# Two transformer layers on one core: transposing queries and keys by block, and moving the buffers of some gated pairs

## The chip, the core and the metric

The kernel runs on one core of a Trainium2 chip. The metric is the device time of one execution in microseconds, and the time before is the median of three. The engines named below are TensorE (PE), VectorE (DVE), ScalarE (ACT), GpSimd (POOL) and SyncE (SP), which issues the large loads.

## What is computed

Two layers over 256 tokens of width 1024, each of a feed-forward half-step, three groups of attention heads side by side, and a second feed-forward half-step, all with scales, shifts and gates from a conditioning vector. Cut to what matters:

```python
def swiglu(h, w_gu, w_down):
    g, u = jnp.split(h @ w_gu, 2, axis=-1)
    return (jax.nn.silu(g) * u) @ w_down

for l in range(DEPTH):                                    # 2
    mod = cond @ w_mod[l] + b_mod[l]
    sh1, sc1, g1, sh2, sc2, g2, sh3, sc3, g3 = jnp.split(mod, 9, axis=-1)
    h = modulate(x, norm_g[l, 0], sh1, sc1)
    x = x + 0.5 * g1[:, None, :] * swiglu(h, w_ffn1_gu[l], w_ffn1_down[l])     # 2 x 2816 wide
    h = modulate(x, norm_g[l, 1], sh2, sc2)
    c_q, c_kv, k_pe, q_s, k_s, v_s, qkv_sb = _split_cols(h @ w_in[l], IN_SIZES)
    qa = (rms_norm(c_q, q_a_norm[l]) @ w_uq[l]).reshape(B, S, MLA_HEADS, MLA_QK)    # 6 heads of 64 + 32
    qa = rms_norm(qa, mla_q_norm[l])
    qa = jnp.concatenate([qa[..., :MLA_NOPE], rope(qa[..., MLA_NOPE:], positions)], axis=-1)
    kv = (rms_norm(c_kv, kv_a_norm[l]) @ w_ukv[l]).reshape(B, S, MLA_HEADS, MLA_NOPE + MLA_V)
    ...                                                   # ka likewise, its rotated part shared by the heads
    o_a = mla_attention(qa, ka, va)
    ...                                                   # o_b: sliding window, o_c: stick-breaking
    x = x + g2[:, None, :] * (mix @ w_out[l])
    h = modulate(x, norm_g[l, 2], sh3, sc3)
    x = x + 0.5 * g3[:, None, :] * swiglu(h, w_ffn2_gu[l], w_ffn2_down[l])
```

## The kernel before

**Matmuls.** Every large product is made of three (`mm3`, L243, L246 and L247): weights and activations are split into a high and a low part (`hi`, `lo`; `h_hi`, `h_lo`), and high x high, high x low and low x high are added up in PSUM. Each is 128x128 weights by 256 tokens, or 258 with two more columns for a shift. ScalarE rounds a loaded weight chunk to its high part (L230), VectorE subtracts to get the low one (L234). PSUM has eight banks, four under the tag `mm` (`pmm`) and four under `acc` (`pacc`).

**Order.** The program is written as generators that advance one another; a scheduler then sets each engine's order from the dependencies. `pin` holds an instruction in the order in which it was written relative to the other pinned ones of its engine. Some orders are written out as numbers (`C`, L27).

**Feed-forward.** There are four such blocks, called FFN 1 to FFN 4 here (two in each layer). The width of 2816 makes 11 pairs j = 0 to 10. A pair's up-projection is gated into a tile `g`, with a high and a low part for two times 128 features, and the down-projection reads it into `acc` banks. The tiles come from the pool `g_p` with three buffers. FFN 1 alone starts with `up_first`, which takes four pairs at once, one eighth of the input width at a time (eight k-steps), since the conditioning vector's scale and shift for each eighth are only then worked out by `opening`: L454 multiplies by the norm's scale, L171 (in `mod_tile`, two for each step) makes scale and shift with L157 and L163 behind it, L460 and L461 on ScalarE apply them and round to `h_hi`, L462 on VectorE gives `h_lo`. Only then can TensorE do the 48 matmuls of the step. Pairs 2 and 3 of FFN 1 lie in two further buffers of their own (`more["g"]`). The other three blocks start with `up_unscaled`, which takes pair 0 on the input before its scale is known, with 258 columns. Between its pairs FFN 1 also makes the table of position biases, with small matmuls at L613.

**Attention.** In each layer the first head group (MLA) makes queries by two matmuls for each block of 128 tokens and three heads (L863), ScalarE and VectorE copy and rotate them into `qcat` (L866, L835 to L838), and VectorE scales the keys from four `mm` banks (`kps`) into `kcat` (L879, L880). Then 24 transposes by TensorE (L900), of 128 tokens by 96, go by twos of heads into an `mm` bank for both blocks; ScalarE copies the queries to `qT` (L903), VectorE the keys to `kT` (L905), 96x512 at a time. Beside it `qv`, a norm of the queries, goes through VectorE (L884), POOL's power (L886) and VectorE again (L888). TensorE has the 258-column matmuls of the next head group (`unscaled`) to go on with, and L1058 makes the scores from `kT` and `qT`. The mixed heads lie in the tiles `mid` until the output projection reads them.

## Time and profile before

| | |
|---|---|
| median of three executions | 1006.03 us (1005.33, 1006.03, 1011.27) |
| the profiled execution | 1007.52 us |
| its span, first to last instruction | 1005.6 us |
| TensorE busy | 983.7 us, 98% of the span |
| VectorE, ScalarE, POOL busy | 792.2, 533.3 and 76.6 us |
| mean granted clock of TensorE | 0.998 |
| read from memory | 242.69 MB, 242 GB/s over the span |

Matmuls are pipelined: one of 256 columns is shown with 0.28 us, and the next starts before it ends. A busy TensorE therefore says nothing of the pace; the number of instructions in a stretch does. The engine's share of busy time is high throughout, so single waits of one or two microseconds are looked for in the order of time.

### The profile page before, as it was taken

Reading aid. Unit: us, or ns where it says so; the run is one execution under the profiler, and the core shown is the slowest. Engines: PE = TensorE matmul, PEld = TensorE weight load, DVE = VectorE, ACT = ScalarE, POOL = GpSimd, SP = SyncE. Lnnn points to the kernel's source line nnn. Section 1 sums busy time; section 2 is a strip of 40 time slices with the busy share of each in tenths; the row PEclk is TensorE's granted clock in tenths of the full one; section 3 lists DMA queues with packets and bytes.
Section 4 is the critical chain, followed back from the end, with each engine's and each line's share of the span. In section 5 each row is a group of like instructions: output and inputs, shape, how many; then the busy total and the mean of one; then the engine's idle time right before and its main releaser. Section 6 shows DMA issues by size and latency. Waiting matters only on the chain.

```text
span 1005.6 us, 20450 instructions
## 1 busy us (share of the span) xinstructions
PE 983.7 (98%) x8396; PEld 957.1 (95%) x8396; DVE 792.2 (79%) x1422; ACT 533.3 (53%) x951; POOL 76.6 (8%) x123
## 2 busy tenths in 40 slices
PE   7999999998999999999999999999999999999998
PEld 6999999997888999999999999999988899999998
DVE  6999788898886898888789877777886678566663
ACT  4464345465755764444376444446575666444442
POOL 6001503002010000000000000000110000000000
PEclk9999999999999999999999999999999999999999
DMA  9988998654661679888866887772443146566631
GB/s 347 414 299 340 296 371 329 271 189 137 224 238 49 244 275 394 340 354 339 348 217 240 335 300 295 273 285 95 127 146 112 58 181 240 194 228 248 224 114 43
DMA packets 47936, 245.13 MB, mean 244 GB/s; under 512 B 4193, under 2 KB 4961, under 8 KB 29666
## 3 DMA queue, kind: packets, MB, share of 16 engines
q1 hardware_dynamic: 47840, 243.81, 64.9%
q8 instruction: 66, 1.08, 0.4%
q14 instruction: 28, 0.23, 0.1%
q10 hardware_dynamic: 2, 0.00, 0.0%
HBM read 242.69 MB, written 1.11 MB: 242 GB/s over the span
## 4 chain that ended last, share of the span: by engine, by line
PE 88%; DVE 7%; ACT 3%; POOL 1%; issue 1%; ACTq 0%; DVEq 0%; POOLq 0%
PE mm L243 16%; PE mm L246 16%; PE mm L247 16%; PE acc L246 11%; PE acc L243 11%; PE acc L247 11%; DVE lo L234 2%; DVE raw L171 1%; PE mm L1102 1%; PE mm L1082 1%; POOL qv L886 1%; PE mm L797 1%; PE mm L613 0%; PE mm L944 0%; PE mm L1143 0%
## 5 line engine op out<-in xcount | busy, mean ns | idle before, releaser
L234 DVE TENSOR_TENSOR lo<-raw,hi 128x1024 fp32r<-128x1024 f32 (+2 forms) x312 | 372.8, 1211 | 115.2 <-ACT hi L230 114.8
L230 ACT ACTIVATE hi<-raw 128x1024 fp32r<-128x1024 f32 (+1 forms) x296 | 306.5, 1048 | 201.9 <-PE mm L246 126.9
L246 PE MATMUL mm<-h_lo,hi 128*128 128x256 f32 (+1 forms) x1360 | 377.1, 278 | 0.0
L243 PE MATMUL mm<-h_hi,hi 128*128 128x256 f32 (+1 forms) x1360 | 376.8, 278 | 0.0
L247 PE MATMUL mm<-h_hi,lo 128*128 128x256 f32 (+1 forms) x1360 | 375.4, 277 | 0.0
L246 PEld LDWEIGHTS mm<-h_lo,hi 128*128 128x128 f32 x1360 | 254.8, 187 | 0.1
L243 PEld LDWEIGHTS mm<-h_hi,hi 128*128 128x128 f32 x1360 | 254.4, 188 | 0.3 <-ACT bias L620 0.2
L247 PEld LDWEIGHTS mm<-h_hi,lo 128*128 128x128 f32 x1360 | 254.0, 187 | 0.2
L243 PE MATMUL acc<-g,hi 128*128 128x256 f32 x682 | 188.9, 277 | 0.0
L247 PE MATMUL acc<-g,lo 128*128 128x256 f32 x682 | 188.9, 277 | 0.0
L246 PE MATMUL acc<-g,hi 128*128 128x256 f32 x682 | 188.7, 277 | 0.0
L171 DVE CUSTOM_DVE_ANT_0 raw<-raw,cond 128x1024 f32<-128x1024 f32 x144 | 172.2, 1220 | 0.0
L247 PEld LDWEIGHTS acc<-g,lo 128*128 128x128 f32 x682 | 128.2, 188 | 0.1
L243 PEld LDWEIGHTS acc<-g,hi 128*128 128x128 f32 x682 | 128.2, 188 | 0.0
L246 PEld LDWEIGHTS acc<-g,hi 128*128 128x128 f32 x682 | 128.0, 188 | 0.0
L243 PE MATMUL acc<-h_hi,hi 128*128 128x256 f32 (+1 forms) x288 | 79.8, 291 | 4.5 <-ACT h_hi L461 1.7
L246 PE MATMUL acc<-h_lo,hi 128*128 128x256 f32 (+1 forms) x288 | 80.5, 285 | 0.2
L247 PE MATMUL acc<-h_hi,lo 128*128 128x256 f32 (+1 forms) x288 | 79.3, 283 | 0.0
L448 ACT ACTIVATE g<-gg 128x256 fp32r<-128x256 f32 x82 | 34.0, 417 | 60.9 <-DVE gg L447 60.8
L445 ACT ACTIVATE sg<-mm 128x256 f32<-128x256 f32 x78 | 29.4, 377 | 59.5 <-PE mm L247 58.9
L243 PEld LDWEIGHTS acc<-h_hi,hi 128*128 128x128 f32 x288 | 53.2, 191 | 6.3 <-ACT h_hi L461 1.9
L246 PEld LDWEIGHTS acc<-h_lo,hi 128*128 128x128 f32 x288 | 54.9, 192 | 0.9 <-DVE h_lo L732 0.6
(307 smaller groups left out, 1122.8 us busy)
## 6 DMA issues: line engine op xcount, KB each, us to landing
raw<-in_dram SPq DMA_DIRECT2D x218, 1024.0 KB, 6.1
raw<-in_dram SPq DMA_DIRECT2D x4, 832.0 KB, 7.3
raw<-in_dram SPq DMA_DIRECT2D x4, 768.0 KB, 4.7
raw<-in_dram SPq DMA_DIRECT2D x4, 512.0 KB, 6.7
far<-relm SPq DMA_DIRECT2D x8, 256.0 KB, 11.4
small<-in_dram SPq DMA_DIRECT2D x2, 960.0 KB, 6.0
xT<-in_dram SPq DMA_DIRECT2D x4, 256.0 KB, 4.2
out_dram<-xT SPq DMA_DIRECT2D x3, 256.0 KB, 2.3
```

The lines of the kernel that those rows point to most:

```text
L171: return DVE.tensor_tensor_reduce(w, w, cond, 1.0, 0.0, ALU.mult, ALU.add, modc[:, l, v, d:d + 1])
L230: t = DVE.tensor_copy(hi, r) if on[i:i + 1] == "d" else ACT.activation(hi, r, AF.Copy)
L234: t = DVE.tensor_tensor(lo, r, hi.bitcast(F32), op=ALU.subtract)
L243: t = PE.matmul(o, wh, ah, start=start, stop=False)
L246: PE.matmul(o, wh, al, start=False, stop=False)
L247: PE.matmul(o, wl, ah, start=False, stop=stop)
L445: ACT.activation(sg, banks[t][:, 0:T], AF.Silu)
L448: behind[0] = ACT.activation(g[:, 0], gg, AF.Copy).ins
L797: PE.matmul(kp[:, 0:384], cT[:, 2, b * P:(b + 1) * P], wukv[:, hf * 384:(hf + 1) * 384], start=True, stop=True)
L886: POOL.tensor_tensor(rq, qv, nhalf[:, 0:12].rearrange("p (a b) -> p a b", a=2), op=ALU.pow)
L1082: PE.matmul(opv[:, i * 64:(i + 1) * 64], pT[:, j * P:(j + 1) * P], va[:, kb, h0 + i], start=kb == 0, stop=kb == b)
L1102: PE.matmul(sp[:, i * P:(i + 1) * P], win["q"][rr, i, b * P:(b + 1) * P], ksT[rr, kb * P:(kb + 1) * P], start=True, stop=True)
```

## The change

It has four parts. In the feed-forward blocks the pool `g_p` has two buffers, not three, and every third pair (j = 0, 3, 6 and 9) lies in a tile `gm` that is 48 floats longer than needed: its data begin after 40 floats where it is j = 0 or FFN 1, else after 48. In the built program that is address 160416 or 160448 in each partition; the second is a multiple of 64, the first lies 32 beyond one. (Before, the three buffers were all at multiples of 64, the two of `more["g"]` 32 beyond; these two, which hold j = 2 and 3 of FFN 1, are so still.) In `opening` L454 is pinned. In attention `qcat` and `kcat` are made earlier in the program, `gr` has a tile of its own, and `lr`, `rk2` and `mx` share those that they are worked out from; through this other tiles move as well, `mid` from 32 beyond a multiple of 64 to a multiple of 64. And the transposes go by block and threes of heads, by the function `turned`: those of the queries into `acc` banks, called as each rotation but the first two has been written, the last two after a block's keys; those of the keys into `mm` banks as each block of `kcat` is written. A copy is then 96x3x128.

```diff
-    g_p = ctx.enter_context(tc.tile_pool(name="g", bufs=3))
+    g_p = ctx.enter_context(tc.tile_pool(name="g", bufs=2))
     act_p = ctx.enter_context(tc.tile_pool(name="act", bufs=1))
+    off_p = ctx.enter_context(tc.tile_pool(name="off", bufs=1))
...
+        def gated(j):
+
+            if j % 3:
+                return g_p.tile([P, 2, 2, T], F32R, tag="g0", name="g")
+            t = off_p.tile([P, 4 * T + 48], F32R, tag="gm", name="gm")
+            return t[:, 40 if start or j == 0 else 48:][:, 0:4 * T].rearrange("p (a b t) -> p a b t", a=2, b=2)
...
-            gt[f0 // 2] = g_p.tile([P, 2, 2, T], F32R, tag="g0", name="g")
+            gt[f0 // 2] = gated(f0 // 2)
...
-                    gt[f // 2] = (more["g"] if t >= 4 else g_p).tile([P, 2, 2, T], F32R, tag="g%d" % max(t - 3, 0), name="g")
+                    gt[f // 2] = more["g"].tile([P, 2, 2, T], F32R, tag="g%d" % (t - 3), name="g") if t >= 4 else gated(f // 2)
...
-            DVE.tensor_tensor(xa[:, d], xT[:, d], rb0, op=ALU.mult)
+            pin(DVE.tensor_tensor(xa[:, d], xT[:, d], rb0, op=ALU.mult))
...
-        gr = gv
+        gr = ap.tile([P, 2, 3], F32, name="gr")
...
+        qss = ap.tile([P, 2, 6], F32, name="qss")
+        kss = ap.tile([P, 2, 6], F32, name="kss")
+        qcat = ap.tile([P, 1536], F32, tag="s1", name="qcat")[:, 0:1152].rearrange("p (b h d) -> p b h d", b=2, h=6)
+        kcat = ap.tile([P, 1536], F32, tag="s2", name="kcat")[:, 0:1152].rearrange("p (b h d) -> p b h d", b=2, h=6)
         kpT = ap.tile([32, T], F32, name="kpT")
...
-        lr = ap.tile([P, 2, 2], F32, name="lr")
+        lr = lv
...
+        def turned(dst, src, b, hf, bank):
+
+            tp = bank()
+            for i in range(3):
+                PE.transpose(tp[0:96, i * P:(i + 1) * P], src[:, b, hf * 3 + i], ident)
+            o = dst[:, hf * 3:hf * 3 + 3, b * P:(b + 1) * P]
+            t3 = heads3(tp[0:96, 0:3 * P])
+            if dst is qT:
+                ACT.activation(o, t3, AF.Copy, scale=gq[0:96])
+            else:
+                DVE.tensor_copy(o, t3)
...
                 DVE.tensor_reduce(qss[:, b, hs], sq, axis=AX.X, op=ALU.add)
+                if 2 * b + hf > 1:
+                    turned(qT, qcat, b - 1, hf, pacc)
...
             DVE.tensor_tensor(kcat[:, b, :, 64:96], krs[b].to_broadcast([P, 6, 32]), spread(rk[:, b], 32), op=ALU.mult)
+            turned(qT, qcat, 1, b, pacc)
+            for hf in range(2):
+                turned(kT, kcat, b, hf, pmm)
...
-        for h2 in range(3):
-            for src, dst in ((qcat, qT), (kcat, kT)):
-                tp = pmm()
-                for i in range(2):
-                    for b in range(2):
-                        PE.transpose(tp[0:96, (i * 2 + b) * P:(i * 2 + b + 1) * P], src[:, b, h2 * 2 + i], ident)
...
-            rk2 = ap.tile([P, 4], F32, name="rk2")
+            rk2 = kv2
...
-        mx = ap.tile([P, 2, 6], F32, name="mx")
+        mx = nm
```

**VectorE in the opening, k-steps 1 and 2, before.** Lines of the kernel after lie 1 above those of the kernel before up to L366 and 8 above them in the feed-forward part: L171 becomes L172, L454 becomes L462 and L462 becomes L470.

```order
L454 TENSOR_TENSOR xa<-xT,rsb 128x256
L171 ISA raw,modc<-raw,cond 128x1024
L171 ISA modc 128x1
L171 ISA raw,modc<-raw,cond 128x1024
L171 ISA modc 128x1
L454 TENSOR_TENSOR xa<-xT,rsb 128x256
L157 TENSOR_TENSOR modc<-modc,cols 128x2
L454 TENSOR_TENSOR xa<-xT,rsb 128x256
L163 SCALAR_TENSOR_TENSOR modc<-modc,cols 128x1
L454 TENSOR_TENSOR xa<-xT,rsb 128x256 x4
L462 TENSOR_TENSOR h_lo<-xa,h_hi 128x256
```

And the same engine after, from the L158 of step 1 on:

```order
L158 TENSOR_TENSOR modc<-modc,cols 128x2
L164 SCALAR_TENSOR_TENSOR modc<-modc,cols 128x1
L470 TENSOR_TENSOR h_lo<-xa,h_hi 128x256
L235 TENSOR_TENSOR lo<-raw,hi 128x1024 x2
L462 TENSOR_TENSOR xa<-xT,rsb 128x256
L172 ISA raw,modc<-raw,cond 128x1024
L172 ISA modc 128x1
L172 ISA raw,modc<-raw,cond 128x1024
L172 ISA modc 128x1
```

The seven products L454 stood nearly together ahead of the first h_lo; now one stands in each step, behind h_lo and the two L235 and ahead of the next L172.

**TensorE in attention of layer 0, before,** from the last query matmuls to the first unscaled one:

```order
L863 MATMUL acc<-small,cT 128x288 x8
L900 MATMUL mm<-ident,qcat 96x128 x4
L900 MATMUL mm<-ident,kcat 96x128
L900 MATMUL mm<-ident,qcat 96x128 x3
L900 MATMUL mm<-ident,kcat 96x128 x3
L900 MATMUL mm<-ident,qcat 96x128
L900 MATMUL mm<-ident,kcat 96x128 x4
L900 MATMUL mm<-ident,qcat 96x128 x4
L900 MATMUL mm<-ident,kcat 96x128 x4
L243 MATMUL acc<-h_hi,hi 128x258
```

After, where L890 is the query matmul, L875 a transpose and L244 the unscaled matmul:

```order
L890 MATMUL acc<-small,cT 128x288 x6
L875 MATMUL acc<-ident,qcat 96x128 x3
L890 MATMUL acc<-small,cT 128x288 x2
L875 MATMUL acc<-ident,qcat 96x128 x9
L875 MATMUL mm<-ident,kcat 96x128 x12
L244 MATMUL acc<-h_hi,hi 128x258
```

The query transposes went into the query matmuls and behind them, into `acc` banks; the key transposes stand together.

**VectorE in attention of layer 1, before,** from the scaling of the keys to the copies of their transposes:

```order
L879 TENSOR_TENSOR kcat<-mm,rkn 128x3x64 x2
L880 TENSOR_TENSOR kcat<-kr,kv 128x6x32
L879 TENSOR_TENSOR kcat<-mm,rkn 128x3x64 x2
L880 TENSOR_TENSOR kcat<-kr,kv 128x6x32
L884 TENSOR_SCALAR qv<-qss,lr_9053 128x6 x2
L293 SCALAR_TENSOR_TENSOR h_lo<-xa,modc,h_hi 128x256
L888 TENSOR_SCALAR qv<-qv,lr 128x6 x2
L905 COPY kT<-mm 96x512 x3
```

After, where L908 and L909 scale the keys, L881 copies transposed keys, L916 and L920 handle `qv`:

```order
L908 TENSOR_TENSOR kcat<-mm,rkn 128x3x64
L909 TENSOR_TENSOR kcat<-kr,kv 128x6x32
L908 TENSOR_TENSOR kcat<-mm,rkn 128x3x64 x2
L881 COPY kT<-mm 96x3x128 x2
L909 TENSOR_TENSOR kcat<-kr,kv 128x6x32
L916 TENSOR_SCALAR qv<-qss,lr_9062 128x6 x2
L294 SCALAR_TENSOR_TENSOR h_lo<-xa,modc,h_hi 128x256
L920 TENSOR_SCALAR qv<-qv,lv 128x6
L881 COPY kT<-mm 96x3x128 x2
L920 TENSOR_SCALAR qv<-qv,lv 128x6
```

Two copies moved ahead of the second block's L909 (L880 before), the other two between the halves of L920, which stood ahead of all copies as L888.

## Rows read from the trace of the kernel before

**Rows 1.** The page: busy time, share of the span and number of instructions of each engine; the granted clock of TensorE in 40 equal slices of the span, in tenths of full speed; shares of the span by engine in the chain of work that ended last.

```profile
PE 983.7 (98%) x8396; PEld 957.1 (95%) x8396; DVE 792.2 (79%) x1422; ACT 533.3 (53%) x951; POOL 76.6 (8%) x123
...
PEclk9999999999999999999999999999999999999999
...
PE 88%; DVE 7%; ACT 3%; POOL 1%; issue 1%; ACTq 0%; DVEq 0%; POOLq 0%
```

**Rows 2.** Busy time of TensorE in nine stretches of the four feed-forward blocks, in which only 128x256 matmuls are issued. Columns: stretch; its length; busy time of TensorE and number of its instructions; granted clock; share of the DMA engines; GB/s. The first six lie in FFN 1, the others in FFN 2, 3 and 4.

```profile
33.00:53.00 20.00, 20.00 (x179) 1.00 1.03 415
61.00:81.00 20.00, 20.00 (x172) 1.00 0.67 242
87.10:98.10 11.00, 11.00 (x97) 1.00 0.86 313
110.00:130.00 20.00, 20.00 (x172) 1.00 1.03 306
147.00:157.00 10.00, 10.00 (x91) 1.00 0.76 287
171.00:191.00 20.00, 20.00 (x173) 1.00 0.87 351
371.00:391.00 20.00, 20.00 (x179) 1.00 0.96 372
555.00:575.00 20.00, 20.00 (x179) 1.00 0.88 343
857.00:877.00 20.00, 20.00 (x179) 1.00 0.56 205
```

**Rows 3.** Single instructions of TensorE in FFN 1, in order of time: start, duration, engine, line, operation, output and inputs, number; in brackets its idle time just before, and what ended it. The first four are of the opening k-steps, the last is of the bias table's matmuls.

```profile
23.06 0.38 PE L243 MATMUL acc<-h_hi,hi 128*128 128x256 f32 x1 [0.72 <-ACT hi L230]
...
30.76 0.50 PE L243 MATMUL acc<-h_hi,hi 128*128 128x256 f32 x2 [1.74 <-ACT h_hi L461]
...
53.55 0.37 PE L246 MATMUL acc<-h_lo,hi 128*128 128x256 f32 x1
...
59.40 0.38 PE L246 MATMUL acc<-h_lo,hi 128*128 128x256 f32 x1
...
143.75 0.88 PE L613 MATMUL mm<-steps,hot 128*128 128x24 bf16 x29
```

**Rows 4.** Single instructions of VectorE near the start, when L454 makes the products of the later k-steps.

```profile
20.07 0.42 DVE L454 TENSOR_TENSOR xa<-xT,rsb 128x256 f32<-128x256 f32 x1
...
20.89 1.42 DVE L454 TENSOR_TENSOR xa<-xT,rsb 128x256 f32<-128x256 f32 x4
22.24 0.41 DVE L462 TENSOR_TENSOR h_lo<-xa,h_hi 128x256 fp32r<-128x256 f32 x1
```

**Rows 5.** Single instructions of VectorE in one k-step of the opening, and the last h_lo.

```profile
38.41 0.16 DVE L163 SCALAR_TENSOR_TENSOR modc<-modc,cols 128x1 f32<-128x1 f32 x1
...
40.19 1.23 DVE L234 TENSOR_TENSOR lo<-raw,hi 128x1024 fp32r<-128x1024 f32 x1 [0.45 <-ACT hi L230]
41.33 0.42 DVE L462 TENSOR_TENSOR h_lo<-xa,h_hi 128x256 fp32r<-128x256 f32 x1
...
44.27 0.16 DVE L163 SCALAR_TENSOR_TENSOR modc<-modc,cols 128x1 f32<-128x1 f32 x1
...
58.92 0.42 DVE L462 TENSOR_TENSOR h_lo<-xa,h_hi 128x256 fp32r<-128x256 f32 x1
```

**Rows 6.** TensorE's instructions that read `mid`, in one stretch of each layer, with the columns of rows 2.

```profile
328.60:337.60 9.00, 9.00 (x78) 1.00 0.38 138
812.10:821.10 9.00, 9.00 (x78) 1.00 0.37 135
```

**Rows 7.** TensorE in attention of layer 0: the first of the last matmuls ahead of the transposes, the first transposes, the first unscaled matmul behind them; then the stretch in which the clock differed, with the columns of rows 2.

```profile
231.72 4.15 PE L863 MATMUL acc<-small,cT 128*128 128x288 f32 x16
239.44 0.61 PE L900 MATMUL mm<-ident,qcat 128*96 128x128 f32 x4 [3.57 <-DVE kcat L879]
...
244.29 0.37 PE L243 MATMUL acc<-h_hi,hi 128*128 128x258 f32 x1
...
240.80:244.20 3.40, 3.40 (x18) 0.50 0.02 5
```

**Rows 8.** VectorE in the same place: the last part of the first block of `kcat`, L888, and the copies of the key transposes; then the one instruction of POOL there.

```profile
239.83 0.35 DVE L880 TENSOR_TENSOR kcat<-kr,kv 128x192 f32<-128x192 f32 x1
...
244.54 0.36 DVE L888 TENSOR_SCALAR qv<-qv,lr 128x6 f32<-128x6 f32 x2 [2.15 <-POOL qv L886]
244.81 1.87 DVE L905 COPY kT<-mm 96x512 f32<-96x512 f32 x3
...
241.33 3.17 POOL L886 TENSOR_TENSOR qv<-qv,nhalf 128x12 f32<-128x12 f32 x1 [4.40 <-DVE qv L884]
```

**Rows 9.** TensorE and VectorE in attention of layer 1: the first and the last transposes of queries and keys, the first matmul of the scores, L888 and the copies of the key transposes.

```profile
730.02 0.63 PE L900 MATMUL mm<-ident,qcat 128*96 128x128 f32 x4
...
732.48 0.60 PE L900 MATMUL mm<-ident,kcat 128*96 128x128 f32 x4
...
736.39 1.10 PE L1058 MATMUL mm<-kT,qT 96*128 96x256 f32 x4 [1.64 <-DVE kT L905]
...
734.10 0.36 DVE L888 TENSOR_SCALAR qv<-qv,lr 128x6 f32<-128x6 f32 x2 [2.16 <-POOL qv L886]
734.37 1.88 DVE L905 COPY kT<-mm 96x512 f32<-96x512 f32 x3
```

More of the change, by code (lines that the diff above doesn't have):

```diff
@@ L823, in attention @@
         DVE.tensor_scalar(kpss, kpss, 1.0 / 96, EPS, op0=ALU.mult, op1=ALU.add)
-        qcat = ap.tile([P, 1536], F32, tag="s1", name="qcat")[:, 0:1152].rearrange("p (b h d) -> p b h d", b=2, h=6)
-        kcat = ap.tile([P, 1536], F32, tag="s2", name="kcat")[:, 0:1152].rearrange("p (b h d) -> p b h d", b=2, h=6)
         va = ap.tile([P, 2, 6, 64], F32, name="va")
-        qss = ap.tile([P, 2, 6], F32, name="qss")
-        kss = ap.tile([P, 2, 6], F32, name="kss")
         ksq = ap.tile([P, 2, 6, 64], F32, tag="s5", name="ksq")
@@ L855, in attention @@
                 ACT.activation(va[:, b, hs], kps[2 * b + hf][:, :, 64:128], AF.Copy, scale=lr[:, 1, b:b + 1])
+        gq = ap.tile([P, 1], F32, name="gq")
+        DVE.memset(gq, 1.0)
+        DVE.tensor_tensor(gq[0:64], c_mq[0:64, l:l + 1], c_mk[0:64, l:l + 1], op=ALU.mult)
+        qT = ap.tile([96, 6, T], F32, name="qT")
+        kT = ap.tile([96, 6, T], F32, name="kT")
+        def turned(dst, src, b, hf, bank):
[8 more added lines that the diff above has]
+                DVE.tensor_copy(o, t3)
         stick_in(0, 3)
```

10 lines of the change are left out of this document (removed).

## The prediction

> **What bounds the kernel now.** I read the page's busy times and its chain of waits first [rows 1]. TensorE is busy for 983.7 of 1005.6 us and holds 88% of the chain; VectorE holds 7%. A gain can therefore come from three things only: the interval at which TensorE issues its matmuls, its granted clock, and the few places where it waits. I looked at each in turn: stretches of nothing but 128x256 matmuls [rows 2], the waits of the opening [rows 3 to 5], the stretches that read `mid` [rows 6], and the places of the transposes in both layers [rows 7 to 9].
>
> The first view holds a surprise. All its stretches are at clock 1.00 and wholly busy, yet they hold different numbers of the same matmul. An instruction that is cut by an edge is counted too, so the interval is (length + 0.28 us) / count: 20.28/179 = 113.3 ns in the stretches at 33, 371, 555 and 857, but 20.28/172 = 117.9 ns at 61 and 110 and 20.28/173 = 117.2 at 171. The window of 147 is fast again: 10.28/91 = 113.0. So FFN 1 runs with two intervals, about 4.5 ns apart, each of which lasts until something breaks the stream; FFN 2, 3 and 4 (371, 555, 857) run at the fast one [rows 2]. A third value belongs to addresses: at 87 to 98 us the gated pairs j = 2 and 3 are read, whose tiles begin 32 bytes beyond a multiple of 64 in the built program, and there it is 11.28/97 = 116.3 ns [rows 2]. `mid`, placed likewise, takes 9.28/78 = 119 ns [rows 6].
>
> **The change part by part.** Everything is summed against the profiled run's own 1007.52 us, which is 1.49 above the median of the three runs, 1006.03.
>
> *L454 in its own k-step.* Before, VectorE did the products for the later k-steps early and nearly together; four in a row took it from 20.89 to 22.24, 0.34 us each [rows 4]. After, each stands ahead of its step's L171. That is on a cycle. From one L163 to the next VectorE needs 44.27 - 38.41 = 5.86 us [rows 5]: L163, ScalarE's part, L234 (which waited 0.45 us for it), h_lo (L462), two L171, L163 again. In the new order L454 stands between h_lo and L171, behind the wait and not beside it, so the cycle becomes 5.86 + 0.34 = 6.20 us. TensorE's share of a step is 48 matmuls at 113.3 ns, 5.44 us. It had been catching up with VectorE throughout and met it at the end: it starts at 53.55 and 59.40 as soon as h_lo is there, the latter begun at 58.92 and 0.42 long [rows 3, 5]. So every delay of the last h_lo is a delay of the end. Step by step: the first later step gets h_hi about 0.4 us sooner, since six products have left its way; the second loses about 0.46 and ends about 0.3 late, because the product for the next step now stands ahead of its L171; from there 0.34 a step over four steps. The last h_lo comes about 0.3 + 4 x 0.34 = 1.65 us later. **+1.65** (bounds +0.5, if ScalarE's part moves up to meet it, and +2.2).
>
> *Transposes, layer 0.* Before, the last L863 ends at 231.72 + 4.15 = 235.87; the first transpose needs a bank that L879 reads last, and starts at 239.44 after 3.57 us of waiting [rows 7]. From 240.8 to 244.2 the granted clock is 0.50, that is 1.2 GHz [rows 7], the one drop in the middle of the kernel; the unscaled matmuls start at 244.29. Layer 1 has no such idle time ahead of its transposes and does 24 of them and two matmuls from 730.02 to 732.48 + 0.60 at full clock, about 3 us where layer 0 takes 4.85 [rows 7, 9]. After, the twelve query transposes go into acc banks as their rotations end, in what was the wait. The key transposes follow L880, which ends for the first block at 239.83 + 0.35; two kT copies, of 3/4 of L905's 0.62 us each, then stand ahead of the second block's L880, and I get the end of the transposes at about 242.95 if the clock stays up: 1.35 us earlier, or nothing at half clock. What is late next is VectorE's L888, which waited 2.15 us for POOL's power [rows 8] and now has the kT copies ahead of it, not behind it; it is done only about 0.6 us ahead of the old last copy (244.81 + 1.87). I take **-0.9** (bounds -1.6 and 0).
>
> The TensorE page of the Trainium skill (TensorE: Matmul & The Clock Gate, Part 4: PE-mode transpose) speaks against this: transposes are said not to count as busy work for the clock, and the full clock not to engage for them. This trace does not bear it out as it stands: the clock rose again at about 244.2, behind a stretch that held nothing but L900's transposes [rows 7]. By the page alone the 1.35 us would not come, and this term would be 0.
>
> *Transposes, layer 1.* Here unscaled matmuls had filled the wait. TensorE then stopped for 1.64 us at L1058 for kT, whose copies ran from 734.37 to 736.25, because L888 stood ahead of them until POOL was done [rows 9]. After, the order has nine unscaled matmuls, six key transposes, eleven more and six more. About 1.9 us of idle time reappears among the query transposes, as fewer unscaled matmuls stand ahead of them; in return nearly all of the pause at L1058 goes. The second block's kT copies stand behind the first of the two L888 still, so kT comes at about 736.3, as before. **+0.2** (bounds -0.5 and +0.8; +1.8 more if the clock falls in the new gap, by layer 0's 4.85 - 3 us).
>
> *Addresses.* In the built program `mid` moves from 32 beyond a multiple of 64 to a multiple of 64. Both layers' 96 reads should go from 119 to 113.3 ns: 192 x 5.7 = 1.1, of which I take **-1.0** (bounds -1.1 and 0). The gated pair j = 0 of FFN 2 to 4 goes the other way, 3 x 48 matmuls by 116.3 - 113.3 = 3 ns: **+0.4**. In FFN 1 j = 0, 6 and 9 do so, **+0.3** (0 to +0.8). h_hi, h_lo, qcat and kcat move too, by multiples of 64 or for short operations: 0. The page "SBUF — State Buffer" of the Trainium skill (Specifications) knows lines of 16 bytes and a price for each crossing; a shift of 32 bytes crosses as many, so by it all these terms would be 0. The two rows differ from it by 3 to 6 ns a matmul [rows 2, 6], and the rows decide.
>
> *The interval in FFN 1.* The slow interval begins behind the last short waits of the opening, at 53.55 and 59.40 [rows 3]. Behind the longer waits at 23.06 (0.72) and 30.76 (1.74) the fast one stands. With a cycle of 6.20 against 5.44 the last waits grow to about 0.76 us, which is nearest to the 0.72 that ended fast. I take the fast interval from there to the bias matmuls at 143.75: 84.35 us less 11.2 of misaligned reads, 73 us x 4.6/117.9 = **-2.8** (bounds -3.6, if the 20 us at 171 turn fast as well, and +0.4, if this stretch stays slow and the 10 us at 147 turn slow too). This is the choice with the thinnest base: two waits of each kind.
>
> *The rest* (separate `gr`, `lr` and `mx` in place, `gq` earlier, small exchanges of order in attention): 0, bounds -1.5 and +1.5, from the waits of 1 to 2 us that such exchanges move [rows 8, 9].
>
> **Sum:** 1.65 - 0.9 + 0.2 - 1.0 + 0.4 + 0.3 - 2.8 = -2.15. 1007.52 - 2.15 = 1005.4 in a run like the profiled one, and 1.49 less against the median: **1003.9**.
>
> **The rivals.**
> *FFN 1 keeps its slow interval.* The 2.8 us don't come: 1006.7. For it: it did so behind both last waits [rows 3]. Against it: these were the shortest.
> *The slow interval reaches FFN 2 to 4: slower.* It is one mechanism with one point of decision. Where the stream of aligned matmuls resumes behind j = 0, whose reads are now misaligned, the interval may be set anew. If it comes out slow, the 1344 later ones of the stage, by the program, each cost 117.9 - 113.3 = 4.6 ns, so about 6 us. One stage gives 1010, two 1016, three 1022. For it: around j = 2 and 3 in FFN 1, slow stands on both sides [rows 2]. Against it: slow stood ahead of them already, so that they need have set nothing.
> *The clock falls still.* Layer 0 gives nothing back, or layer 1 falls too: 1003.9 + 0.9, or 1.8 more, so 1004.8 to 1006.6. For it: a 3.57 us wait led to a drop and transposes run through it [rows 7]; against it: waits of 1.74 and 1.64 didn't [rows 3, 9]. [...]
> *The opening doesn't lose.* If the products fall into VectorE's 0.45 us wait after all, with layer 0's gain whole: 1003.9 - 1.65 - 0.5 = 1001.8.
>
> **How the numbers follow.** Forecast 0.40; slow FFN 1 0.22; clock 0.10; no loss in the opening 0.12; slow interval in later stages 0.16, of which one stage has half and two or three the other half. The range takes the first four with their bounds (about 1000 up to 1007) and one slow stage (1010 plus its spread): **1000 to 1011**. About 1% is what a measurement of this kernel can tell from no change: the bounds are 996 and 1016. Below 996 no case reaches; 0.06 for what I have not seen. Above 1016 are two or three slow stages, 0.08, and some unseen wait, 0.03. Faster 0.06, same 0.83, slower 0.11.
>
> **What would show it.** L454 once in each step, and the last h_lo at about 60.6. Query transposes from about 235.9 on with no clock of 0.50 behind them, and unscaled matmuls from about 243. L1058 at about 736.5, moved by what came before it. `mid` at 113 to 114 ns, j = 0 of FFN 2 to 4 at 116 to 117. The stretches at 61 and 110 with 179 matmuls in 20 us. I am wrong if a window of 20 us in FFN 2 to 4 shows 172, if TensorE waits over 3 us among the transposes, or if the opening ends sooner than before.

## The result, and the profile after

The kernel after takes **1025.23 us** (median of four executions: 1023.03, 1028.24, 1027.43, 1015.21), the kernel before in the same comparison 1005.72 (1005.33 to 1011.27). The ratio is 1.0141, an estimate from the fast executions of both that is not the quotient of the two medians, with a 95% interval from 1.0091 to 1.0191: slower by some 1%, and 14 us above the range of 1000 to 1011. A second comparison on another chip gave 1.0081 (1.0036 to 1.0126). The times of every kernel here, also of the one before, vary by 10 to 25 us from one execution to the next with the share of time in which TensorE runs at 1.2 GHz. So beside the ratios I use the **full-clock time**, an estimate: the span times the mean granted clock of the same execution, as a mean over all executions with its standard error. It takes off somewhat too much, since it halves time at 1.2 GHz also where TensorE waits for another engine: over the executions of before, a microsecond of lost clock costs 0.74 to 0.90 us by a straight-line fit in each group. In the second comparison it is 1006.6 ± 1.0 (12 executions) against 1002.3 ± 0.3 (29): 4.3 us more, where the forecast had 2.15 less.

The profiled execution took 1023.03 us, with a span of 1021.0 and a mean clock of 0.991. Its page, with the rows that answer to [rows 1]:

```profile
PE 993.9 (97%) x8396; PEld 965.1 (95%) x8396; DVE 793.9 (78%) x1424; ACT 533.0 (52%) x953; POOL 78.6 (8%) x123
...
PEclk9999999998999999999999999999989999999999
```

These totals hardly differ from [rows 1]: VectorE has 1.7 us more work, TensorE 10.2 us more busy time in as many instructions. A view by stretches says where. The stretches of [rows 2], columns as there:

```profile
33.00:53.00 20.00, 20.00 (x177) 1.00 1.03 401
61.00:81.00 20.00, 19.91 (x174) 1.00 0.64 231
87.10:98.10 11.00, 11.00 (x96) 1.00 0.94 325
110.00:130.00 20.00, 20.00 (x179) 1.00 1.02 315
147.00:157.00 10.00, 10.00 (x89) 1.00 0.79 297
171.00:191.00 20.00, 20.00 (x179) 1.00 0.85 345
371.00:391.00 20.00, 20.00 (x179) 1.00 0.97 363
555.00:575.00 20.00, 20.00 (x172) 1.00 0.93 360
857.00:877.00 20.00, 20.00 (x177) 1.00 0.70 257
```

FFN 1 has turned fast at 110 and 171 (x179, was x172 and x173). FFN 3, at 555, has turned slow (x172, was x179). The x177 at 857 is no slow interval: the stretch now holds the misaligned pair j = 0 of FFN 4.

The two programs have the same number of matmuls, so the n-th of one can be set against the n-th of the other. The lag of the kernel after grows so:

| part | matmuls by number | lag grows by | forecast |
|---|---|---|---|
| to the end of the opening | 0 to 405 | +1.9 | +1.65 |
| rest of FFN 1 | 405 to 1900 | -2.9 | -2.5 |
| attention, layer 0 | 1900 to 2300 | +5.6 | -0.9 |
| `mid`, FFN 2, start of FFN 3 | 2300 to 4400 | -0.6 | -0.4 |
| rest of FFN 3 | 4400 to 5900 | +6.1 | +0.1 |
| attention, layer 1 | 5900 to 6200 | +5.3 | +0.2 |
| to the end (`mid` again, FFN 4) | 6200 to 8395 | 0.0 | -0.4 |
| sum | | +15.4 | -2.2 |

**FFN 3.** TensorE and VectorE where the first gated pair is read:

```profile
542.69 1.22 DVE L172 CUSTOM_DVE_ANT_0 raw<-raw,cond 128x1024 f32<-128x1024 f32 x1
...
543.83 1.22 DVE L172 CUSTOM_DVE_ANT_0 raw<-raw,cond 128x1024 f32<-128x1024 f32 x1
...
544.98 1.22 DVE L235 TENSOR_TENSOR lo<-raw,hi 128x1024 fp32r<-128x1024 f32 x1
...
545.93 0.28 PE L244 MATMUL acc<-gm,hi 128*128 128x256 f32 x1
546.04 0.28 PE L247 MATMUL acc<-gm,hi 128*128 128x256 f32 x1
546.25 0.39 PE L248 MATMUL acc<-gm,lo 128*128 128x256 f32 x1
546.48 0.28 PE L244 MATMUL acc<-gm,hi 128*128 128x256 f32 x1
```

L248 starts 0.21 us behind L247, not 0.12, and the next L244 0.23 behind L248: it reads `lo`, which L235 has ready at 544.98 + 1.22 = 546.20, late because two L172 stand ahead of it on VectorE. I call this a stumble; TensorE isn't shown idle in it. Behind this misaligned pair all 1344 aligned matmuls go at 117.8 ns. FFN 2 and FFN 4 have no such stumble; their j = 0 goes at 117.4 ns and what follows at 113.3. The kernel before stumbles at the same place, inside an aligned pair, and what follows goes at 113.3:

```profile
541.04 1.22 DVE L234 TENSOR_TENSOR lo<-raw,hi 128x1024 fp32r<-128x1024 f32 x1
...
542.10 0.28 PE L246 MATMUL acc<-g,hi 128*128 128x256 f32 x1
542.31 0.39 PE L247 MATMUL acc<-g,lo 128*128 128x256 f32 x1
```

**Attention, layer 1.** TensorE and VectorE from the query transposes to the next head group, then two stretches of TensorE. They answer to [rows 9]; L900 is now L875, L905 L881, L888 L920, L1058 L1073:

```profile
732.06 3.18 PE L890 MATMUL acc<-small,cT 128*128 128x288 f32 x12
...
736.05 0.50 PE L875 MATMUL acc<-ident,qcat 128*96 128x128 f32 x3 [0.81 <-ACT qsq L896]
...
746.77 1.05 PE L1073 MATMUL mm<-kT,qT 96*128 96x256 f32 x4
...
750.75 1.19 PE L959 MATMUL mm<-cqk 64*128 64x128 f32 x6 [2.05 <-ACT cqk L775]
...
745.42 0.23 DVE L920 TENSOR_SCALAR qv<-qv,lv 128x6 f32<-128x6 f32 x1 [2.16 <-POOL qv L918]
...
746.63 2.06 DVE L294 SCALAR_TENSOR_TENSOR h_lo<-xa,modc,h_hi 128x256 fp32r<-128x256 f32 x5
748.61 1.21 DVE L235 TENSOR_TENSOR lo<-raw,hi 128x1024 fp32r<-128x1024 f32 x1
749.74 0.74 DVE L774 TENSOR_TENSOR ct<-acc,rsb 128x256 f32<-128x256 f32 x2
...
747.60:751.00 3.40, 1.35 (x14) 1.00 0.12 17
751.00:754.40 3.40, 3.40 (x18) 0.50 0.72 292
```

The pause at the scores is gone, as forecast. But TensorE now waits 2.05 us for `cqk`, the scaled queries and keys of the next head group. ScalarE makes them from `ct`, and `ct` stands on VectorE behind five L294 and an L235, which piled up in L920's 2.16 us wait for POOL. From the first query matmul to the first on `cqk` there are 750.75 - 732.06 = 18.69 us, before 737.97 - 721.98 = 15.99:

```profile
721.98 4.15 PE L863 MATMUL acc<-small,cT 128*128 128x288 f32 x16
...
737.97 0.88 PE L944 MATMUL mm<-cqk 64*128 64x128 f32 x6
```

Then the clock is at 1.2 GHz up to 757.8, behind a stretch in which TensorE was busy for 1.35 us of 3.40; that is +3.3. This part is drawn: of the seven traces with this wait, five have 3.4 or 6.8 us at 1.2 GHz in the hundred matmuls from 6100 on, two (gated pairs aligned, later tick) have none.

**Attention, layer 0**, which answers to [rows 7]; L863 is now L890:

```profile
230.66 3.18 PE L890 MATMUL acc<-small,cT 128*128 128x288 f32 x12
236.72 0.50 PE L875 MATMUL acc<-ident,qcat 128*96 128x128 f32 x3 [2.88 <-ACT qsq L896]
237.06 1.14 PE L890 MATMUL acc<-small,cT 128*128 128x288 f32 x4
...
243.32 1.52 PE L875 MATMUL mm<-ident,kcat 128*96 128x128 f32 x6 [1.05 <-DVE kcat L909]
244.49 0.56 PE L244 MATMUL acc<-h_hi,hi 128*128 128x258 f32 x1
...
240.80:244.20 3.40, 1.74 (x10) 0.74 0.28 113
244.20:249.20 5.00, 5.00 (x25) 0.50 0.00 0
```

The wait has not been filled: the query transposes need an `acc` bank which ScalarE's L896 has to read first, and four query matmuls stand behind them. The unscaled matmuls start 13.83 us after the first query matmul, before 12.57. The clock was at 1.2 GHz for 6.8 us from 242.4 on (before 3.4 us from 240.8), so that it now falls on the unscaled matmuls too.

**The opening**: TensorE's wait in the second later k-step, and VectorE's last steps, which answer to [rows 3, 5]:

```profile
31.69 0.74 PE L244 MATMUL acc<-h_hi,hi 128*128 128x256 f32 x4 [2.75 <-ACT h_hi L469]
...
51.81 0.16 DVE L164 SCALAR_TENSOR_TENSOR modc<-modc,cols 128x1 f32<-128x1 f32 x1
...
58.02 0.16 DVE L164 SCALAR_TENSOR_TENSOR modc<-modc,cols 128x1 f32<-128x1 f32 x1
...
60.94 0.42 DVE L470 TENSOR_TENSOR h_lo<-xa,h_hi 128x256 fp32r<-128x256 f32 x1
```

The cycle is 58.02 - 51.81 = 6.21 us (forecast 6.20), the last `h_lo` begins at 60.94 (forecast about 60.6).

**`mid`**, with the columns of [rows 6]:

```profile
331.00:340.00 9.00, 8.91 (x79) 1.00 0.57 213
826.50:835.50 9.00, 8.97 (x76) 1.00 0.50 190
```

Both are aligned now, but only layer 0 has gained: start to start its matmuls take 113.6 ns, those of layer 1 117.8; before, both took 118.3.

### The profile page after: what moved, and what is told of

Read it like the earlier page. It is cut to its first block, busy times and chain, and to the rows that moved or that the text cites. A ratio compares the mean times of both kernels' runs of the same rounds, so it can differ in the third digit from the quotient of the medians.

```text
span 1021.0 us, 20454 instructions
## 1 busy us (share of the span) xinstructions
PE 993.9 (97%) x8396; PEld 965.1 (95%) x8396; DVE 793.9 (78%) x1424; ACT 533.0 (52%) x953; POOL 78.6 (8%) x123
## 4 chain that ended last, share of the span: by engine, by line
PE 87%; DVE 6%; ACT 3%; DMA 2%; POOL 1%; issue 1%; SPq 0%; POOLq 0%; DVEq 0%
PE mm L244 15%; PE mm L247 15%; PE mm L248 15%; PE acc L247 12%; PE acc L248 11%; PE acc L244 11%; DVE lo L235 2%; DVE raw L172 2%; PE mm L959 1%; PE mm L1097 1%; PE mm L1117 1%; DMA cols<-in_dram 1%; ACT hi L231 1%; PE mm L1073 1%; DMA raw<-in_dram 1%
## 5 line engine op out<-in xcount | busy, mean ns | idle before, releaser
L235 DVE TENSOR_TENSOR lo<-raw,hi 128x1024 fp32r<-128x1024 f32 (+2 forms) x312 | 372.7, 1210 | 120.0 <-ACT hi L231 119.6
L247 PE MATMUL mm<-h_lo,hi 128*128 128x256 f32 (+1 forms) x1360 | 377.6, 278 | 0.0
L244 PE MATMUL mm<-h_hi,hi 128*128 128x256 f32 (+1 forms) x1360 | 377.1, 279 | 0.0
L248 PE MATMUL mm<-h_hi,lo 128*128 128x256 f32 (+1 forms) x1360 | 376.2, 278 | 0.0
L248 PEld LDWEIGHTS mm<-h_hi,lo 128*128 128x128 f32 x1360 | 255.0, 188 | 0.2
L247 PEld LDWEIGHTS mm<-h_lo,hi 128*128 128x128 f32 x1360 | 254.8, 187 | 0.1
L244 PEld LDWEIGHTS mm<-h_hi,hi 128*128 128x128 f32 x1360 | 254.0, 187 | 0.2
L172 DVE CUSTOM_DVE_ANT_0 raw<-raw,cond 128x1024 f32<-128x1024 f32 x144 | 172.0, 1219 | 0.0
L244 PE MATMUL acc<-g,hi 128*128 128x256 f32 x450 | 125.0, 278 | 0.0
L247 PE MATMUL acc<-g,hi 128*128 128x256 f32 x450 | 125.0, 278 | 0.0
L248 PE MATMUL acc<-g,lo 128*128 128x256 f32 x450 | 124.9, 278 | 0.0
L244 PE MATMUL acc<-h_hi,hi 128*128 128x256 f32 (+1 forms) x288 | 81.4, 295 | 5.0 <-ACT h_hi L469 2.7
L248 PEld LDWEIGHTS acc<-g,lo 128*128 128x128 f32 x450 | 85.0, 189 | 0.0
L247 PEld LDWEIGHTS acc<-g,hi 128*128 128x128 f32 x450 | 84.5, 188 | 0.0
L244 PEld LDWEIGHTS acc<-g,hi 128*128 128x128 f32 x450 | 84.5, 188 | 0.0
L247 PE MATMUL acc<-h_lo,hi 128*128 128x256 f32 (+1 forms) x288 | 81.7, 289 | 0.4
L248 PE MATMUL acc<-h_hi,lo 128*128 128x256 f32 (+1 forms) x288 | 80.6, 287 | 0.0
L244 PE MATMUL acc<-gm,hi 128*128 128x256 f32 x232 | 64.8, 279 | 0.0
L248 PE MATMUL acc<-gm,lo 128*128 128x256 f32 x232 | 64.7, 279 | 0.0
L247 PE MATMUL acc<-gm,hi 128*128 128x256 f32 x232 | 64.6, 279 | 0.0
L244 PEld LDWEIGHTS acc<-h_hi,hi 128*128 128x128 f32 x288 | 54.8, 196 | 6.5 <-ACT h_hi L469 3.1
```

The lines of the kernel that those rows point to most:

```text
L172: return DVE.tensor_tensor_reduce(w, w, cond, 1.0, 0.0, ALU.mult, ALU.add, modc[:, l, v, d:d + 1])
L235: t = DVE.tensor_tensor(lo, r, hi.bitcast(F32), op=ALU.subtract)
L244: t = PE.matmul(o, wh, ah, start=start, stop=False)
L247: PE.matmul(o, wh, al, start=False, stop=False)
L248: PE.matmul(o, wl, ah, start=False, stop=stop)
```

## The experiments

Each kernel is told as a change to the kernel after or before. The kernels of one group share a chip and the executions of before: 1013.33 us (31 of them) in the first group, 1010.18 (29) in the second, 1015.9 (29) in the third, 1010.5 (17) in the last.

### First group: parts undone, one part alone

**After, all gated pairs of `gm` aligned.**

```diff
-            return t[:, 40 if start or j == 0 else 48:][:, 0:4 * T]...
+            return t[:, 48:][:, 0:4 * T]...
```

> The kernel after with every gm tile beginning at a multiple of 64 bytes (offset 48 in all cases); the order of every engine is unchanged. Theory 1 (a stumble inside a misaligned pair leaves the slow interval behind it): FFN 3 has 179 matmuls in the 20 us at 555, as before, instead of 172; the later stage ends 6 us sooner, and j = 0 costs 0.5 us less, so about 1016 to 1018 where the kernel after has about 1023 to 1025. Rival (the interval is drawn by chance at any stumble, aligned or not): FFN 3 slow again in some runs, and the time unchanged within its spread. Both: the attention stages stay as they are, 10 us slower than before.

Measured: 1013.73 us, ratio 1.0022 (0.9972 to 1.0072); full clock 1004.1 ± 0.7 against 1001.8 ± 0.4. FFN 3 is at x179 in its stretch, though the stumble is still there; FFN 1 is slow again in one stretch (x173 at 61). One trace does not show that misalignment is needed for the slow FFN 3; the count over all traces stands below. About 2 us of the loss are left without it. Attention is 3.5 us longer than in the kernel before, not 10: most of what the kernel after lost there more was time at 1.2 GHz.

**After, the transposes as before.**

```diff
-                if 2 * b + hf > 1:
-                    turned(qT, qcat, b - 1, hf, pacc)
...
+        for h2 in range(3):
+            for src, dst in ((qcat, qT), (kcat, kT)):
+                tp = pmm()
```

> The kernel after with the transposes as before (after all of qcat and kcat, by twos of heads, in mm banks); pinned L454, misaligned pairs and moved tiles stay. Theory 2 (the transposes by block stretch a thinly filled time of TensorE, so that the granted clock falls for longer and in both layers): the 10.3 us that attention lost go, one drop of 3.4 us is left in layer 0 as before, none in layer 1, about 1013 to 1015. Rival (the moved tiles and the exchanges of order behind the transposes cost it): attention keeps at least half of the loss, 1018 to 1023.

Measured: 1017.78 us, ratio 1.0013 (0.997 to 1.0055); full clock 1003.0 ± 1.3, in two groups: six executions at 998.0 to 1002.7, four at 1006.8 to 1009.1. Its trace has FFN 3 slow (x172 at 555) and attention as before: matmuls 6000 to 6200 take 30.22 us (before 30.20, after 35.47), and matmuls 1900 to 2300, in layer 0, 62.17 (before 62.03, after 67.62). So the loss in layer 1 belongs to the transposes, the FFN 3 loss does not; layer 0 differs too much between traces to be told from these three (below). Two groups some 7 us apart, in one program, are what an interval drawn in each execution would give.

**After, L454 (now L462) not pinned.**

```diff
-            pin(DVE.tensor_tensor(xa[:, d], xT[:, d], rb0, op=ALU.mult))
+            DVE.tensor_tensor(xa[:, d], xT[:, d], rb0, op=ALU.mult)
```

> The kernel after with L454 not pinned. Theory 3 (the pinned product lengthens each k-step): the opening ends about 1.7 us sooner, near 63.4 instead of 65.2 at the four-hundredth matmul. What FFN 1 does behind it decides the rest: if its interval is fast again, 1.7 us off the total; if slow as in the kernel before, about 1 us is added. So 1022 to 1026.

Measured: 1019.82 us, ratio 1.002 (0.9967 to 1.0074); full clock 1007.9 ± 1.0. The four-hundredth matmul starts at 65.11, hardly sooner than after (65.16), so this sign failed; counted from matmul 20, which came later in this execution, the opening to 405 takes 52.73 us, after 53.35. TensorE's wait in the second later step is 1.75 us, as in the kernel before, not 2.75 as after. Over all traces, matmuls 20 to 405 take 53.8 us on the mean of eight traces with the pin (53.3 to 54.6) and 52.3 on the mean of six without (51.9 to 53.1): 1.5 us for the pin. Some of it may be the clock's: seven of the eight show 3.4 or 6.8 us at 1.2 GHz from about 31 to 33 us on, one of the six does, and the kernel after, without such a drop, takes 53.4. That the full-clock time is nonetheless the highest of all these kernels is not explained; its FFN 3 stumbles and is fast in the trace, and its executions spread from 1002.9 to 1012.6.

**Before, with the new transposes alone.**

```diff
+                if 2 * b + hf > 1:
+                    turned(qT, qcat, b - 1, hf, pacc)
...
+            turned(qT, qcat, 1, b, pacc)
+            for hf in range(2):
+                turned(kT, kcat, b, hf, pmm)
```

> The kernel before with the transposes by block and threes of heads alone; no tile moves. Theory 2: attention loses what it lost in the kernel after, 5 us in layer 0 and 5 in layer 1, by clock drops of 6.8 us: about 1015 to 1017. FFN 2 to 4 at the fast interval throughout. Rival (the moved tiles matter): 1006 to 1010.

Measured: 1015.07 us, ratio 1.0024 (0.9976 to 1.0071); full clock 1004.8 ± 0.7, that is 3.0 us more than before. In layer 1 matmuls 6000 to 6100 take 18.02 us (before 16.01), the whole of attention 3.1 us more in layer 0 and 5.4 in layer 1. The transposes cost time on their own, by the full-clock time and by layer 1; the ratio alone would allow none.

### Second group: the point of decision, and the wait in layer 1

**The kernel after again, unchanged.**

> The kernel after, unchanged, with many runs beside as many of the kernel before, since the four runs of it spread from 1015 to 1028 and runs of the kernel before on another chip spread as far. Theory (the change costs some 6 us of full-speed time, and the rest of the 19.5 us was the draw of the clock in those runs): span times mean granted clock has a median near 1008 where the kernel before has 1002; times of both spread over 15 us, and the ratio is 1.004 to 1.010. Rival (the change itself costs 1.4% or more): 1.014 and above, and span times clock at 1015.

Measured: 1021.65 us (1013.23 to 1030.5), the second comparison told above: the ratio of 1.0081 is in the theory's range, and the rival's 1.014 above the interval. FFN 3 is slow again in its trace.

**After, FFN 3's shift work begun one tick later**, so that no L172 stands ahead of that L235; TensorE's order is the same.

```diff
-    def ticker(*tasks):
+    def ticker(*tasks, first=0.0):
-        due = [0.0] * len(tasks)
+        due = [first] * len(tasks)
...
-            ffn(l, 0, w_gu1[l], w_down1[l], (l, 1), ticker((ms, R4)))
+            ffn(l, 0, w_gu1[l], w_down1[l], (l, 1), ticker((ms, R4), first=-1.0))
```

> The kernel after with the first two reductions of the conditioning vector in FFN 3 one tick later, so that they don't stand on VectorE ahead of the low weights of the down-projection of j = 0; TensorE's order is unchanged and the pair is misaligned still. Theory (the slow interval came from a stumble of 0.1 us inside the misaligned pair): no interval over 200 ns at the start of j = 0 of FFN 3, and 179 matmuls in 20 us behind it, as in FFN 2 and 4. Rival (it is the misaligned pair alone, with a chance in each stage): slow in FFN 3 as often as in two of three traces so far.

Measured: 1013.32 us, ratio 1.0022 (0.9987 to 1.0057); full clock 1005.4 ± 0.4, the narrowest spread of all (1003.8 to 1008.2; after, 1001.7 to 1014.8). VectorE in the same place and TensorE at the first reads of `gm`, then the stretch at 555:

```profile
543.07 1.22 DVE L235 TENSOR_TENSOR lo<-raw,hi 128x1024 fp32r<-128x1024 f32 x1
...
547.78 0.28 PE L244 MATMUL acc<-gm,hi 128*128 128x256 f32 x1
547.89 0.28 PE L247 MATMUL acc<-gm,hi 128*128 128x256 f32 x1
548.01 0.28 PE L248 MATMUL acc<-gm,lo 128*128 128x256 f32 x1
...
555.00:575.00 20.00, 20.00 (x179) 1.00 0.84 324
```

`lo` is ready over 3 us ahead, L248 follows L247 by 0.12 us, and FFN 3 is fast. Over the traces of all kernels, FFN 3 with misaligned pair and stumble was slow in three of seven (after, after again, transposes as before); with stumble and aligned pair it was fast in six of six; and no stretch behind a misaligned pair without stumble (FFN 2, FFN 4, this one) was slow. So the slow interval is drawn, and behind a misaligned pair it took the stumble: 3 of 7 with it, 0 of 17 without. That it also takes the misalignment is likely, not shown: if aligned pairs were as prone, none in six would still come out about once in eight times (all ways of spreading three such stretches over thirteen). The outcome shows right behind the stumble, before the aligned stream resumes: the rest of the misaligned pair itself goes at 117.3 to 117.4 ns in the three traces that turn slow, and at 118.5 to 118.7 in the four that stay fast. Why it falls one way or the other stays open.

**After, the query transposes of block 0 behind the loop.**

```diff
-                if 2 * b + hf > 1:
-                    turned(qT, qcat, b - 1, hf, pacc)
...
+        for hf in range(2):
+            turned(qT, qcat, 0, hf, pacc)
```

> The kernel after with the first block's query transposes called behind the loop over the query matmuls, so that TensorE issues all eight of these first; banks, copies and all else stay. Theory (the last pair of query matmuls stood behind three transposes that waited for an acc bank until ScalarE had read it, and so the last rotations, kcat and the key transposes came 2 us late): from the six-thousandth matmul to the next hundredth 16.0 to 16.4 us as in the kernel before, instead of 18.0; in layer 0 the unscaled matmuls start about 12.5 us behind the first query matmul, instead of 14. Rival (the copies of the query transposes on ScalarE and the key copies on VectorE cost it): 17.5 to 18.0 still.

Measured: 1027.04 us, ratio 1.0113 (1.0042 to 1.0183), four executions. Matmuls 6000 to 6100 take 17.84 us, hardly less than after (18.00), and `ct` is still behind five L294. For layer 1 the theory that the last query matmuls, standing behind the waiting transposes, cost the time has fallen. In layer 0 the unscaled matmuls start 12.89 us behind the first query matmul (forecast 12.5, after 13.83); but the other traces with the unchanged transposes have 11.4 to 13.6 there, so this shows nothing.

**Before, with the pin alone.** The edit is the reverse of that of "L454 not pinned" above.

> The kernel before with L454 pinned and nothing else. Theory: from the matmul numbered 20 to the one numbered 405 the opening takes 53.3 to 54.3 us where it takes 51.9 in the kernel before (and 52.7 and 53.1 in the two other runs without the pin), so 1 to 1.5 us more; the wait for the second later step's h_hi is 2.6 to 2.8 us, not 1.7 to 1.9. Attention and FFN 2 to 4 as in the kernel before. Rival (the opening's length is set by the interval that is drawn, not by the pin): the wait as before, and a length of 52 to 53 us.

Measured: 1013.64 us, ratio 1.0039 (0.9997 to 1.0082); full clock 1003.0 ± 0.7 against 1002.3 ± 0.3. That is no proof of the pin's 1.5 us, nor against it. In its trace the wait is 2.74 us and matmuls 20 to 405 take 54.6, as the theory had it (the length 0.3 above its range, with 3.4 us at 1.2 GHz in it). The trace shows something else as well: two stretches of TensorE in layer 0's attention.

```profile
303.00:313.00 10.00, 9.42 (x45) 0.50 0.12 52
313.00:323.00 10.00, 10.00 (x41) 0.50 0.00 0
```

The clock is at 1.2 GHz for some 20 us on end, where the kernel before and the kernel after are both at 2.4 GHz in their traces. This program has neither new transposes nor moved tiles. Five other traces have the same stretch.

### Third and last groups: the wait in layer 1, FFN 1, and a faster version

**After, layer 1's L920 (before: L888) issued behind `ct`.**

```diff
-                DVE.tensor_tensor(t, banks[j][h][:, 0:T], rsb, op=ALU.mult)
+                last[0] = DVE.tensor_tensor(t, banks[j][h][:, 0:T], rsb, op=ALU.mult).ins
...
+        if l:
+            with tc.issue_after(last[0]):
+                for b in range(2):
+                    DVE.tensor_scalar(rq[:, b], rq[:, b], lr[:, 0, b:b + 1], 96.0 ** -0.5, ...)
```

> The kernel after with VectorE's last step on qv in layer 1 (two instructions of 0.2 us that wait 2.2 us for POOL) queued behind the products ct; three low parts of h then stand behind ct, not ahead of it. Theory (in layer 1 the loss is a new wait of 2.05 us at the first matmuls on cqk, since ct stood on VectorE behind five low parts that had piled up while it waited for POOL): no such wait, and from the first query matmul to the first matmul on cqk 15.8 to 16.2 us as in the kernel before (15.99), instead of 18.1. Rival (TensorE's idle time among the query transposes is the loss): 17.5 to 18.1 still. The total can't show 2 us within its spread; FFN 3 slow in about half of the executions.

Measured: 1018.59 us, ratio 1.0069 (1.0027 to 1.0111); full clock 1005.4 ± 1.3 against 1003.5 ± 0.5. TensorE in layer 1 (L959 is L965 here):

```profile
733.98 3.18 PE L891 MATMUL acc<-small,cT 128*128 128x288 f32 x12
...
749.95 0.85 PE L965 MATMUL mm<-cqk 64*128 64x128 f32 x6
```

The wait is gone: 749.95 - 733.98 = 15.97 us, not 18.69. The new wait for `cqk` thus comes from the order on VectorE. The idle time among the transposes is still there: matmuls 6000 to 6100 take 18.00.

**Before, with the misaligned pairs and the moved tiles alone.** The diff is the first three pieces of the change, and its tile edits.

> The kernel before with the misaligned pairs and the moved tiles alone: transposes as before, L454 not pinned; TensorE's order is that of the kernel before. Theory: FFN 1 fast in each stretch behind its misaligned pairs (2 to 3 us less than the kernel before), FFN 3 slow in about three executions of five (6 us more), FFN 2 and 4 fast; span times clock therefore falls into two groups, near 999 and near 1005, where the kernel before has 1002. Rival (the slow FFN 3 comes with the transposes or the pin): FFN 3 fast always, one group near 999.

Measured: 1015.85 us, ratio 1.0001 (0.9955 to 1.0047); full clock 1004.3 ± 1.3 against 1003.5 ± 0.5, again in two groups: four executions at 998.9 to 1001.4, five at 1006.7 to 1009.0, one at 1004.1. In its trace all of FFN 1 is fast (matmul 1700 starts at 199.89, before 202.25) and FFN 3 stumbles but is fast. The theory's 2 to 3 us in FFN 1 are too much, though: matmuls 405 to 1900 take 154.8 to 155.5 us in the nine traces with misaligned pairs, 157.8 in that of the kernel before, but 155.2 to 156.1 in the four other traces with aligned ones. On the mean that is 0.9 us, against a risk of 6 in FFN 3.

**A faster version: before, misaligned pairs in FFN 1 only, and L888 behind `ct` in layer 1**; no pin, transposes as before.

```diff
+            return t[:, 40 if start else 48:][:, 0:4 * T]...
...
+        if l:
+            with tc.issue_after(last[0]):
```

> What the runs so far recommend: the kernel before with pairs 0, 6 and 9 misaligned in FFN 1 alone, aligned in FFN 2 to 4, with the moved tiles, and with VectorE's last step on qv in layer 1 behind ct; transposes as before, L454 not pinned. Theory: FFN 1 at the fast interval behind its misaligned pairs (2 to 3 us), FFN 3 fast always, and in layer 1 no wait for kT (1.6 us): span times clock near 998, where the kernel before has 1002; ratio 0.996. Rival (these gains drown or are paid back, in a wait for h_lo in layer 1): 1001 to 1002.

Measured: **1007.11 us** (1002.6 to 1020.2, 12 executions) against 1015.9 of before, ratio **0.9954 (0.9911 to 0.9997)**; full clock 999.5 ± 1.0 against 1003.5 ± 0.5. The interval of the ratio ends just below 1. FFN 1 and FFN 3 in its trace:

```profile
110.00:130.00 20.00, 20.00 (x179) 1.00 1.02 309
...
555.00:575.00 20.00, 20.00 (x179) 1.00 0.86 336
```

Ten of its executions have 995.1 to 1000.6 us at full clock, two 1005.8 and 1007.3. These two lie as far off as one slow stage would put them, with all pairs of FFN 2 to 4 aligned; no trace of them was kept, so that aligned pairs keep FFN 3 fast always is not shown.

**Before, with L888 behind `ct` in layer 1 alone.**

> The kernel before with one edit: in layer 1 the last step of the query norm (L888 there, behind POOL's power) is issued behind the scaling of the next head group's queries (L763, ct), as in the faster version; layer 0, the gated pairs and the transposes are as before. Theory (VectorE's wait for POOL holds up the copies of the keys and ct, and nothing else takes its place): from the first query matmul to the first matmul on cqk in layer 1 there are 14.1 us, not 15.99, and no pause of 1.64 us at the scores; at full clock the kernel is about 1.9 us shorter than before, and the faster version's other part, the misaligned pairs of FFN 1, is worth only the rest of its 4 us. Rival (the pause only moves on to the next wait of TensorE behind the scores, and the faster version owes its gain to FFN 1): that stretch is shorter, but by the matmuls of the next head group the lead is below 0.5 us, and the full-clock time is that of the kernel before within 0.7 us.

Measured: 1008.21 us against 1010.5, ratio 0.9969 (0.9932 to 1.0007); full clock 1000.0 ± 0.5 against 1002.3 ± 0.5, so 2.3 ± 0.7 less; the ratio's interval still holds 1. TensorE in layer 1:

```profile
730.73 4.15 PE L864 MATMUL acc<-small,cT 128*128 128x288 f32 x16
...
744.82 0.38 PE L950 MATMUL mm<-cqk 64*128 64x128 f32 x2
```

No wait at the scores, and 744.82 - 730.73 = 14.09 us to `cqk`, 1.9 less than before. VectorE's wait for POOL had been the cost at this place all along; the new transposes had moved it from one reader to another. With the same cure the new transposes need 15.97 us to `cqk`, the old ones 14.09, so the idle time among the new ones is a loss of its own. What remains of the faster version's gain is 1.7 us with an error of 1.3, from two different chips; FFN 1 is 0.35 us shorter there than in this trace (matmuls 405 to 1900), so its part is not shown.

## Why the prediction was wrong

**Right.** *L454 in its own step*: +1.65 forecast, +1.5 by the traces with and without the pin; the cycle came out to 0.01 us. *The interval of FFN 1* with its misaligned reads: -2.5 forecast, -2.9 in the trace. That was luck: of 14 traces, the one that the forecast was read from is the only one with all of FFN 1 up to the bias matmuls slow once the opening ends, and against the other traces with aligned pairs the gain is under 1 us on the mean (told with the misaligned pairs alone). The reason given was wrong, too. I laid it to longer last waits of the opening; the kernel with misaligned pairs and no pin keeps FFN 1 fast without them. In the three stretches between and behind the bias matmuls, FFN 1 was fast in all nine traces with misaligned pairs and slow in 7 of 15 stretches with aligned ones. *j = 0*: 117.4 ns for 116.3 forecast.

**The forecast failed at five steps.**

1. *"Where the stream of aligned matmuls resumes behind j = 0 ... the interval may be set anew."* This rival came true in one stage of the profiled execution, at the price given (6.1 for "about 6"), but its point of decision was put in the wrong place and its chance (0.16) was too small. It isn't the resuming that decides: FFN 2 and 4 resume in the same way and stay fast. It is a stumble of 0.1 us inside the misaligned pair, which stands in the kernel before too (VectorE has L171 ahead of that L234 there), and was harmless in all six traces in which the pair is aligned. I had looked at the waits of the opening only, since a stumble is not shown as idle time.

2. *Transposes, layer 1, +0.2*: it was +2.0, and in this trace +3.3 more by the clock. The idle time among the transposes and the end of the pause at L1058 came as told. The step that failed is "in return nearly all of the pause at L1058 goes": I followed the key copies past L888 and stopped there. The five L294, the L235 and the `ct` behind them on VectorE were in the same order of instructions; the next reader down that queue became the one to wait. The experiment with L920 behind `ct` shows it: 15.97 us to `cqk`, not 18.69.

3. *Transposes, layer 0, -0.9*: in this trace the unscaled matmuls start 1.3 us later, and attention is 5.6 longer. It has 10.2 us at 1.2 GHz there, before had 3.4; half of the difference, 3.4 us, is the clock's, and 2.2 are left. Over all traces it is less: with half the time at 1.2 GHz taken off, matmuls 1900 to 2300 take 60.0 to 62.5 us in the eight with the new transposes (mean 61.1) and 60.0 to 60.5 in the six with the old ones (mean 60.3), so about +0.8, and the unscaled matmuls start no later on the mean (12.5 and 12.8 us behind the first query matmul). The gain of 0.9 did not come. The step "into acc banks as their rotations end, in what was the wait" failed: the banks come free only when ScalarE has read them (2.88 us of waiting), and four query matmuls now stand behind. What exactly sets the length of this place stays open. The upper bound, 0, was too near.

4. *`mid`, -1.0*: alignment gives 113.6 ns only where the interval is the fast one. In 15 of 20 aligned stretches over the traces the mean was 117.1 to 117.8, against 118.2 to 118.4 misaligned; over all 20 it is 116.6. The term is then 192 x 1.7 ns, about -0.3. I had taken the fast interval for the property of an aligned address, though [rows 2] showed both at aligned addresses.

5. *One execution taken for the kernel.* The profiled execution had a mean clock of 0.998 and one drop in its middle [rows 7]; later executions of the same kernel, on four chips, had 0.979 to 0.998, and went up to 1029 us. Of the 15.4 us between the two profiled executions, about 7 are clock. About 6 more are the slow FFN 3, which not every execution has. Over the twelve executions of the second comparison the change is some 4 us at full clock; the ratio of 1.014 had a draw of the clock in it, which no step of mine could have told, but for which the range left no room. The rival on the clock came true in both layers of this trace, at 3.4 and 3.3 us where it had 0.9 and 1.8.

## What to carry to other kernels

When an instruction is moved past a wait, follow that engine's queue behind it until an instruction that somebody else needs, and price that reader: here the wait for POOL went from the scores to the next head group, while the cure was to put the waiting instruction itself behind all urgent ones. Before a stretch of equal matmuls is called fast or slow, count them in windows in several executions; where both values turn up, treat it as a draw and ask what starts it. A short start-to-start gap of TensorE that the profile shows as busy can set the pace of the next 150 us.
